# A decoder layer in split float32: every SBUF tile is laid 32 bytes further

## The chip, the core and the metric

The kernel runs on one core of one Trainium2 chip. The metric is the device time of one launch in microseconds (us). Before the change, three runs gave 2425.56, 2427.79 and 2438.43 us, a median of 2427.79.

## The reference, cut to what matters

One decoder layer for 1,024 tokens of width 1,024, all in float32:

```python
f1 = swiglu(rms_norm(h, g1), ffn1_w_in, ffn1_w_out)      # 1024 -> 2 x 2816 -> 1024
h  = h + 0.5 * rms_norm(f1, p1)
u  = rms_norm(h, mix_pre_g)
p_rwkv, p_swa, q_mem, gate_logits = split(u @ w_in)      # 1792 | 768 | 512 | 3 x 1024 columns
y_a = rwkv7_mix(p_rwkv, ...)                             # a recurrence over the tokens
y_b = sliding_window_gqa_sinks(q_s, k_s, v_s, sinks)     # window 128
y_c = memory_cross_attention(q_mem, rms_norm(mem), mem_w_kv)
g_a, g_b, g_c = split(sigmoid(gate_logits + gate_b))
merged = g_a * (y_a @ wb0) + g_b * (y_b @ wb1) + g_c * (y_c @ wb2)
h  = h + rms_norm(merged @ w_out, mix_post_g)
f2 = swiglu(rms_norm(h, g2), ffn2_w_in, ffn2_w_out)
h  = h + 0.5 * rms_norm(f2, p2)
```

## The kernel before, in words

Activations lie feature by feature: a tile of 128 features by 512 tokens (half of the tokens) is 2,048 bytes in each of the 128 partitions. Weights come from HBM in strips of 128 x 1,024 values, 4,096 bytes in each partition, into two buffers named `w_raw` (line 121).

The large products keep float32 accuracy with a cheaper type, float32r. `operand` (lines 125 to 131) casts half a strip to a float32r tile `w_hi` on ScalarE and puts what the cast lost into a tile `w_lo` on VectorE. `split` (lines 248 to 251) does the same for activations, into pairs of tiles of the pool `u`. `mm3` (lines 190 to 196) then multiplies three times: high weights by high activations (L194), high weights by low activations (L195), low weights by high activations (L196). Each of these matmuls streams an activation tile, in most cases 512 columns wide, past 128 x 128 weights; each loads its weights anew.

The smaller products of the mixer (the recurrence in `rwkv_chain`, the two attentions, the sums over a head) use plain float32. The trace counts two matmul instructions for one of these in the program, and one for a float32r matmul or a transpose.

The stages follow one another: the memory's keys and values, the first feed-forward block, the mixer (preparation and inversion for the recurrence, the recurrence itself, attention over memory and over the window, gates, branches), the output projection, the second feed-forward block. In both feed-forward blocks the products of `ffn_in_pair` (names `px`, `py`, `pz`) come first, and those of `ffn_out_one` (`po`) after. `plan` (line 81) lists the strips in the order of use, and `prefetch` makes operands up to eight ahead. A scheduler orders the instructions of each engine by that program and its priorities.

Where a tile lies is settled by the pools. Pools on the left side grow up from byte 16,512 of a partition, pools on the right side grow down from the top; every tile takes a multiple of 32 bytes. On the left stand the constants (pool `consts`: `vecs` with 488 bytes, `ones`, `ident`, `post1`, `post2`), then the weights (pool `w`: `w_raw`, `w_hi`, `w_lo`, `w_sum`), then the pools of each stage. On the right stand the pool `u` with 32 tiles, and the pool `quarters` with the tiles named `acc`, `r2`, `f`, `hid` and `x_re`. In the mixer many stage tiles stand behind constants of odd sizes.

Of the kernel before, what the change touches and what calls it, by code (L numbers as in the profile page):

```python
# [10 lines left out]
F32 = mybir.dt.float32  # L11
# [6 lines left out]
P = 128  # L18
# [58 lines left out]
class Builder:  # L77
# [1111 lines left out]
    def build(self):  # L1189
        nc, tc, io = self.nc, self.tc, self.io  # L1190
        with contextlib.ExitStack() as outer, tc.tile_pool(reuse_waits="tile", name="consts", bufs=1) as cp, \
             tc.tile_pool(reuse_waits="tile", name="w", bufs=1) as self.wpool, \
             tc.tile_pool(reuse_waits="tile", name="pmm", bufs=8, space=bass.MemoryType.PSUM) as self.pmm:
            self.plan()
            self.vecs = cp.tile([P, NVEC], F32, name="vecs")
            nc.scalar.dma_start(self.vecs, io["vecs"])
            self.ones = cp.tile([P, 1], F32, name="ones")
# [14 lines left out]
            vm_d = tc.dram_tile([P, 2, 512], F32, name="vm_d")  # L1212
            hid_d = tc.dram_tile([KF, P, T], F32, name="hid_d")
            first_d = tc.dram_tile([max(FIRST.values()), 2, P, TH], F32, name="first_d")
            self.upool = outer.enter_context(tc.tile_pool(reuse_waits="tile", name="u", bufs=32, side="right"))
            quarters = lambda: tc.tile_pool(reuse_waits="tile", name="quarters", bufs=16, side="right")
            u = self.new_u()
# [122 lines left out]
```

## Time and profile before

| | |
|---|---|
| median of three runs | 2427.79 us (2425.56 to 2438.43) |
| profiled execution, first to last instruction (span) | 2422.9 us |
| TensorE (PE): matmuls busy | 98% of the span, 12,500 matmul instructions |
| weight loads (PEld) busy | 79% |
| VectorE (DVE) busy | 64% |
| ScalarE (ACT) busy | 37% |
| GpSimd (POOL) busy | 4% |
| mean granted TensorE clock | 0.995 |
| DMA | 323.75 MB, mean 134 GB/s |

The profiled execution's own time is its span of 2422.9 us and whatever lies around it; the median of the runs is 4.9 us above the span.

How to read the rows below. PE is a matmul, PEld the weight load that belongs to it; DVE, ACT and POOL are the three vector-like engines. L194 is line 194 of the kernel. `po<-u,w_hi` names the output and the operands; of a matmul the first operand named is the one that streams past the weights. `x640` counts instructions. Matmuls overlap one another in the pipeline, so a matmul's duration is longer than the step from one start to the next; that step is what sets the pace.

### The profile page before, as it was taken

To read this page: it belongs to the slowest core of one execution; us is meant where nothing else is said; L and a number is where in the kernel's file an instruction comes from. 1 tells how busy PE (TensorE), PEld (TensorE's weight loads), DVE (VectorE), ACT (ScalarE), POOL (GpSimd) and SP (SyncE) were. 2 spreads that over 40 slices of the span, in tenths; PEclk is the share of its full clock that TensorE was granted. 3 is DMA by queue.
4 is the path that set the end of the run, shared out by engine and by line. 5 is a ranking of instruction groups with operands and counts; after the bars stand their busy time and mean duration, and the time that the engine had idled before them with its cause. 6 is when DMAs were issued, how large, how long until landed. Compare 5 with 4: busy or idle time off the path is not lost.

```text
span 2422.9 us, 33132 instructions
## 1 busy us (share of the span) xinstructions
PE 2367.7 (98%) x12500; PEld 1926.0 (79%) x12500; DVE 1550.3 (64%) x2563; ACT 895.5 (37%) x1680; POOL 107.7 (4%) x145
## 2 busy tenths in 40 slices
PE   7999999999999999999999999999999999999998
PEld 6878888788888777887777877778887778878888
DVE  8976555654588775993435366575897665564535
ACT  6523333422345533223344464334642233341221
POOL 2000000000000000001210000240000000000000
PEclk9999999999999999999999999999999999999999
DMA  7453222632344244225326434555545432252303
GB/s 253 148 187 114 95 79 79 195 112 84 103 156 146 96 163 168 97 112 177 115 82 209 126 115 136 169 178 170 171 159 177 158 107 91 90 190 97 113 22 105
DMA packets 159615, 323.75 MB, mean 134 GB/s; under 512 B 31296, under 2 KB 61504, under 8 KB 159200
## 3 DMA queue, kind: packets, MB, share of 16 engines
q1 hardware_dynamic: 144000, 294.31, 36.6%
q10 hardware_dynamic: 15456, 27.33, 3.3%
q8 instruction: 98, 1.61, 0.3%
q14 instruction: 61, 0.50, 0.1%
HBM read 231.41 MB, written 89.13 MB: 132 GB/s over the span
## 4 chain that ended last, share of the span: by engine, by line
PE 79%; DVE 10%; DMA 5%; issue 3%; ACT 3%; POOL 0%; ACTq 0%; SPq 0%; DVEq 0%; POOLq 0%
PE po L194 6%; PE po L195 6%; PE po L196 6%; PE px L194 5%; PE px L195 5%; PE px L196 5%; PE pgate L194 3%; PE pgate L196 3%; PE pgate L195 3%; DMA w_raw<-in_ffn_in 2%; PE pz L195 2%; PE pz L194 2%; PE pz L196 2%; DVE w_lo L131 2%; PE pr L196 2%
## 5 line engine op out<-in xcount | busy, mean ns | idle before, releaser
L129 ACT CAST w_hi<-w_raw 128x512 fp32r<-128x512 f32 x560 | 343.2, 620 | 837.5 <-PE po L195 216.6
L131 DVE TENSOR_TENSOR w_lo<-w_raw,w_hi 128x512 fp32r<-128x512 f32 x552 | 387.4, 705 | 165.8 <-ACT w_hi L129 159.3
L194 PE MATMUL po<-u,w_hi 128*128 128x512 f32 (+2 forms) x768 | 288.9, 376 | 2.3 <-DVE acc L492 2.3
L196 PE MATMUL po<-u,w_lo 128*128 128x512 f32 (+2 forms) x768 | 288.2, 375 | 0.0
L195 PE MATMUL po<-u,w_hi 128*128 128x512 f32 (+2 forms) x768 | 288.1, 375 | 0.0
L495 DVE TENSOR_TENSOR acc<-po,acc 128x512 f32<-128x512 f32 (+2 forms) x136 | 89.5, 658 | 177.6 <-PE po L196 177.4
L194 PEld LDWEIGHTS po<-u,w_hi 128*128 128x128 f32 x768 | 144.4, 188 | 29.0 <-DVE acc L492 4.1
L196 PEld LDWEIGHTS po<-u,w_lo 128*128 128x128 f32 x768 | 144.4, 188 | 25.0
L195 PEld LDWEIGHTS po<-u,w_hi 128*128 128x128 f32 x768 | 144.4, 188 | 24.7
L194 PE MATMUL pgate<-u,w_hi 128*128 128x512 f32 x384 | 154.3, 402 | 0.0
L196 PE MATMUL pgate<-u,w_lo 128*128 128x512 f32 x384 | 153.7, 400 | 0.0
L195 PE MATMUL pgate<-u,w_hi 128*128 128x512 f32 x384 | 153.1, 399 | 0.0
L194 PE MATMUL px<-f,w_hi 128*128 128x512 f32 x352 | 138.2, 393 | 6.9 <-DVE u L406 3.8
L195 PE MATMUL pz<-u,w_hi 128*128 128x512 f32 x352 | 136.9, 389 | 0.5 <-DVE u L251 0.5
L195 PE MATMUL px<-u,w_hi 128*128 128x512 f32 x352 | 137.2, 390 | 0.0
L196 PE MATMUL px<-u,w_lo 128*128 128x512 f32 x352 | 137.2, 390 | 0.0
L196 PE MATMUL px<-f,w_lo 128*128 128x512 f32 x352 | 137.1, 390 | 0.0
L195 PE MATMUL px<-f,w_hi 128*128 128x512 f32 x352 | 137.0, 389 | 0.0
L194 PE MATMUL pz<-u,w_hi 128*128 128x512 f32 x352 | 136.9, 389 | 0.0
L196 PE MATMUL pz<-u,w_lo 128*128 128x512 f32 x352 | 136.9, 389 | 0.0
L194 PE MATMUL px<-u,w_hi 128*128 128x512 f32 x352 | 136.9, 389 | 0.0
L260 ACT ACTIVATE sq<-acc 128x512 f32<-128x512 f32 (+2 forms) x104 | 60.9, 598 | 106.2 <-DVE acc L495 88.8
(324 smaller groups left out, 4713.8 us busy)
## 6 DMA issues: line engine op xcount, KB each, us to landing
w_raw<-in_ffn_in SPq DMA_DIRECT2D x110, 512.0 KB
w_raw<-in_win SPq DMA_DIRECT2D x56, 512.0 KB
w_raw<-in_ffn_out SPq DMA_DIRECT2D x52, 512.0 KB
hid_d<-g SPq DMA_DIRECT2D x88, 256.0 KB
hid<-hid_d SPq DMA_DIRECT2D x88, 256.0 KB
gate_d<-gate SPq DMA_DIRECT2D x24, 512.0 KB
pk_d<-pk ACTq DMA_DIRECT2D x4, 2560.0 KB
f<-pk_d SPq DMA_DIRECT2D x16, 640.0 KB
```

Source lines behind the costliest of these rows:

```text
L129: self.nc.scalar.copy(hi, x)
L131: (engine or self.nc.vector).tensor_tensor(lo, x, hi.bitcast(F32), ALU.subtract)
L194: mm(out, wh, xh, start=first, stop=False, **kw)
L195: mm(out, wh, xl, start=False, stop=False, **kw)
L196: mm(out, wl, xh, start=False, stop=last, **kw)
L260: nc.scalar.activation(sq, x, ACT.Square)
L495: self.nc.vector.tensor_tensor(out, ps, out, ALU.add)
```

## The change

Two tiles of 32 bytes in each partition are added, which nothing reads or writes. One, `pad`, is the first tile of the constants and pushes every tile on the left 32 bytes up. The other, `edge`, is the first tile of the right side and pushes every tile there 32 bytes down.

```diff
             self.plan()
+            cp.tile([P, 8], F32, name="pad")
             self.vecs = cp.tile([P, NVEC], F32, name="vecs")
...
             first_d = tc.dram_tile([max(FIRST.values()), 2, P, TH], F32, name="first_d")
+            outer.enter_context(tc.tile_pool(name="edge", bufs=1, side="right")).tile([P, 8], F32, name="edge")
             self.upool = outer.enter_context(tc.tile_pool(reuse_waits="tile", name="u", bufs=32, side="right"))
```

In the two built programs every engine has the same instructions in the same order with the same waits. Of 3,156 tile instances in SBUF, 2,535 lie 32 bytes higher, 616 lie 32 bytes lower, and 5 (constants of the framework) stay. Tiles in PSUM and tensors in HBM stay where they were. What is left of some starting bytes when they are divided by 128:

| tiles | before | after |
|---|---|---|
| `w_raw`, `w_hi`, `w_lo`, `w_sum`; `m1`, `g`, `up` of the feed-forward blocks; memory tiles `mem_x`, `mem_hi`, `mem_lo`; `y` of the last branch | 96 | 0 |
| `u`, `acc`, `r2`, `hid`, `x_re`, and `f` of the feed-forward blocks | 96 | 64 |
| `lora`, `g_up`, `bones`, `center`, `gmask`, `wmask` | 96 | 0 |
| `ident` | 32 | 64 |
| the mixer's stage tiles: `pk`, `f`, `gz`, `bk`, `uv`, `sv`, `z` of the recurrence; `qs`, `sc`, `pt`, `km_in`, `vm_in`, `kd`, `vt`, `cos`, `sin`; `gate`, `att` | 0 | 32 |
| `yin` | 64 | 96 |

So the tiles of the feed-forward blocks and all float32r operands lie at multiples of 64 bytes after the change, and most of the mixer's own tiles, which did so before, no longer do.

## The prediction

> **What bounds the kernel now.** I read the page first, then the table by stretches, then the order of time on TensorE.
>
> ```profile
> span 2422.9 us, 33132 instructions
> PE 2367.7 (98%) x12500; PEld 1926.0 (79%) x12500; DVE 1550.3 (64%) x2563; ACT 895.5 (37%) x1680; POOL 107.7 (4%) x145
> PE 79%; DVE 10%; DMA 5%; issue 3%; ACT 3%; POOL 0%; ACTq 0%; SPq 0%; DVEq 0%; POOLq 0%
> ```
>
> TensorE is busy for 98% of the span, and 79% of the chain that ended last is its work. In whole stretches it never rests, at the full granted clock, with every other engine below it:
>
> ```profile
> 300.00:400.00 100.00, 100.00 (x443) 82.81 (x442) 55.82 (x87) 36.58 (x63) 0.00 (x0) 1.00 0.26 88
> 1000.00:1100.00 100.00, 100.00 (x443) 82.81 (x442) 87.60 (x104) 23.42 (x39) 0.00 (x0) 1.00 0.35 129
> ```
>
> The columns behind the two times are PE, PEld, DVE, ACT and POOL, the granted clock, the DMA share and GB/s. So what counts is the step from one matmul to the next. The order of time on PE from 320 to 330 us has 46 rows, of which these are the first and the last:
>
> ```profile
> 319.72 0.39 PE L194 MATMUL px<-u,w_hi 128*128 128x512 f32 x1
> ...
> 329.92 0.39 PE L194 MATMUL px<-f,w_hi 128*128 128x512 f32 x1
> ```
>
> 45 steps in 10.20 us are 226.7 ns each. Three rows, one for each line of `mm3`, count the float32r matmuls:
>
> ```profile
> 0.00:2423.00 2423.00, 1215.59 (x3136) 590.43 (x3136) 0.99 0.40 134
> 0.00:2423.00 2423.00, 1213.64 (x3136) 590.54 (x3136) 0.99 0.40 134
> 0.00:2423.00 2423.00, 1215.93 (x3136) 590.54 (x3136) 0.99 0.40 134
> ```
>
> 3 x 3,136 = 9,408 of them; at 226.7 ns they would take 2,133 us, nearly the whole span. A change of one nanosecond in this step is worth up to 9.4 us.
>
> **What the change can touch.** It moves no instruction, adds none and adds no wait; the order of work on every engine is the same. Only starting addresses differ: operands of the float32r matmuls go from odd multiples of 32 bytes to multiples of 64, and the mixer's own tiles go the other way. So the question for each engine is whether its instructions care about 32 bytes. The trace of before holds tiles of both kinds, so most of this can be read off.
>
> VectorE and ScalarE: each pair has first an instruction all of whose SBUF tiles lie at odd multiples of 32 (remainder 96 by 128), then one of the same shape whose tiles lie at multiples of 64.
>
> ```profile
> L424 DVE TENSOR_TENSOR g<-g,up 128x512 f32<-128x512 f32 x44 | 30.4, 690 | 3.9 <-ACT g L423 1.4
> L910 DVE TENSOR_TENSOR qs<-qs,cos 128x512 f32<-128x512 f32 x8 | 5.5, 689 | 6.2 <-DMA qs<-att_d 5.9
> L260 ACT ACTIVATE sq<-acc 128x512 f32<-128x512 f32 x88 | 54.3, 631 | 55.8 <-DVE acc L495 38.4 <-DVE sq L264 8.5 <-DVE acc L523 7.8
> L798 ACT ACTIVATE ysq<-y 128x512 f32<-128x512 f32 x8 | 4.8, 629 | 0.1
> ```
>
> 690 against 689 ns and 631 against 629 ns (some of the 88 tiles `sq` lie at multiples of 64 too). I cost both engines at nothing. Even if the 1 or 2 ns were real, they run beside a TensorE that is never idle in the stretches above.
>
> Plain float32 matmuls: `ps_rs<-ident,rsy` streams `ident`, which lies at remainder 32, and `mpv<-mpt,vm_in` streams `mpt`, at remainder 0. Both are 128 columns wide:
>
> ```profile
> L244 PE MATMUL ps_rs<-ident,rsy x100: 271/275/550, 26.2 to 2415.7; 128*128 128x128 f32 x100
> L1033 PE MATMUL mpv<-mpt,vm_in x128: 272/275/377, 1342.5 to 1408.0; 128*128 128x128 f32 x128
> ```
>
> The median is 275 ns for both. So I cost the mixer's tiles, which lose their multiple of 64, at nothing. The bound on the other side stands under the rivals.
>
> DMA: no row tells transfers to the two kinds of tile apart. It is 5% of the chain, about 120 us, so a tenth more or less on each transfer would be 12 us at most; I take nothing, because in the stretches above the DMA engines are busy for a quarter to a third of the time.
>
> The float32r matmuls are what stays open, because in the kernel before every one of them streams a tile at remainder 96. What can be worked out is how much of their step is not columns. Plain float32 matmuls that stream tiles at remainder 0 give the price of a column:
>
> ```profile
> 815.93 1.88 PE L683 MATMUL rk<-m,bones 128*128 128x512 f32 x4
> L683 PE MATMUL rk<-m,bones x16: 590/592/593, 815.9 to 942.8; 128*128 128x512 f32 x16
> 1344.34 1.89 PE L1012 MATMUL msc<-km_in,qm 128*128 128x256 f32 x8
> L1012 PE MATMUL msc<-km_in,qm x64: 379/379/382, 1334.4 to 1400.7; 128*128 128x256 f32 x64
> ```
>
> The first row of each pair is a merged group from first start to last end, the second has the median duration of one. (1.88 - 0.592) / 3 steps = 429 ns for 512 columns; (1.89 - 0.379) / 7 = 216 ns for 256. The difference is 0.832 ns a column, so 429 - 426 = 3 ns is a remainder that belongs to the instruction. If float32r runs its columns at twice that pace, 0.416 ns, 512 columns are 213 ns, and 226.7 leaves a remainder of 13.7 ns. It does not grow with the width. These are the first and the last of 17 rows with 384 columns:
>
> ```profile
> 2353.33 0.33 PE L195 MATMUL po<-u,w_hi 128*128 128x384 f32 x1
> ...
> 2356.11 0.33 PE L196 MATMUL po<-u,w_lo 128*128 128x384 f32 x1
> ```
>
> 2.78 us / 16 = 173.8 ns, less 384 x 0.416 = 159.7, leaves 14.1 ns. So each float32r matmul carries about 13.7 ns that plain float32 at remainder 0 does not show: 10.7 ns more. Either float32r itself or the address is the reason, and no row separates them. The bounds are therefore 0 and 10.7 x 9,408 = 101 us less, and nothing suggests a longer step except the rival below.
>
> I take 0, for three reasons from the rows. First, none of the three comparisons above shows an effect of 32 bytes. Second, plain float32 takes a column in twice the time, so whatever supplies a float32r matmul has half the time for each, and a remainder of its own is what I would expect of it. Third, 13.7 ns are 13.7 / 0.416 = 33 columns, or about 128 bytes. If that were one more piece of an operand that does not start on a piece, the piece would be 128 bytes, and the activations still start at remainder 64 after the change; the extra piece would stay.
>
> A rule of the Trainium skill speaks against the change here too: SBUF — State Buffer, section Specifications, gives lines of 16 bytes and a penalty for crossing to a new one. By that rule a tile at a multiple of 32 starts on a line before and after, and the step stays at 226.7 ns. No row of this trace shows the size of a line.
>
> The sum is then 0 on every engine: the span stays at 2422.9 us and the median at about 2427 us.
>
> **The rivals.**
>
> Rival A, the address makes the remainder. Operands at multiples of 64 bytes let float32r drop to a remainder of 3 ns, a step of 216 ns. For it: the remainder is the same for every width, as a cost at the start of a stream would be. Against it: the three reasons above. It would give 10.7 x 9,408 = 101 us if every float32r matmul were on the path; with the chain's 79% it is 80 us. I take 90: 2338 us, between 2326 and 2348. If only half of the remainder goes (one of two costs, at the weights or at the stream), it is 45 us: 2383 us. The Trainium skill supports A: TensorE: Matmul & The Clock Gate, section "Wait — 56ns, not 53.3ns?", states about 2.5 ns as the fixed cost of back-to-back matmuls. By that rule 11.2 ns of the 13.7 come from somewhere else, which would be 105 us; the 3 ns of the float32 rows agree with it, the float32r rows do not.
>
> Rival B, ending slower: the two reads of TensorE fall out of step. The matmul's stream and the next matmul's weight load read SBUF at the same time. Before, weights and activations have the same remainder, 96; after, 0 and 64. After each stall the trace shows a slower pace that settles only after some ten matmuls:
>
> ```profile
> 61.83 0.40 PE L194 MATMUL py<-r,w_hi 128*128 128x512 f32 x1
> ...
> 64.14 0.39 PE L195 MATMUL px<-u,w_hi 128*128 128x512 f32 x1
> ```
>
> Ten steps in 2.31 us are 231 ns, 4.3 ns over the settled 226.7. If settling needs equal starts and no longer happens, the kernel loses 4.3 x 9,408 = 40 us: about 2468 us. It decides from the point where the settled step is over 228 ns (1.3 x 9,408 = 12 us). Against it: the weight load takes its place beside the stream in plain float32, with operands at remainders 0 and 96 (`m` and `bones`), at a remainder of only 3 ns.
>
> Rival C, the change doesn't do what it says: the streamed activations lie at multiples of 64, but not of 128, and the mixer's tiles lose what the others gain. Where 128 bytes are the unit, only the 192 matmuls that stream `y` in the last branch and the 144 of the memory's keys and values would get faster: 336 x 10.7 ns, under 4 us. That is within no change, and I count it there.
>
> **How the numbers follow.** A measurement of this kernel can tell about 0.5%, 12 us, from no change. No change, C among it: 0.57. A: 0.31, of which 0.19 for the full and 0.12 for the half. B and a loss in the mixer that the rows above don't show: 0.12. The likeliest is no change, 2427 us; its own range is 2420 to 2440, about the spread of the three runs. The range that is to hold 8 in 10 has to take in A, since A has more than 2 in 10: it reaches from 2326 us, the full gain on every matmul, to 2440, and leaves out B.
>
> **What would show it.** In the profile after, the step of `px` and `po` at 512 columns settles it: 226 to 227 ns says that the remainder is float32r's own (or has a unit of 128 bytes), 216 ns says A, 220 to 222 the half, over 228 B. A step that is shorter for `pb<-y` (remainder 0) than for `pb<-u` (64) says 128 bytes. The medians of 690, 631 and 275 ns should stand as they are; if `mpv`, which then streams tiles at remainder 32, went above 275 ns, my costing of the mixer would be wrong. The prediction is wrong if the time leaves 2415 to 2440 us; a shorter time with an unchanged step would mean that DMA or the other engines held the kernel up where I saw none.

## The result, and the profile after

The changed kernel is slower: 2466.11 us median of four runs (2465.31 to 2471.59) against 2427.89 us (2425.56 to 2438.43), a ratio of 1.0151 with a 95% interval of 1.0129 to 1.0174. That is the number of rival B (2468 us), to which the prediction gave a part of 0.12, and it lies outside the range.

The page of the changed kernel, the lines that answer to those of before:

```profile
span 2469.5 us, 33132 instructions
PE 2420.0 (98%) x12500; PEld 1930.6 (78%) x12500; DVE 1553.1 (63%) x2563; ACT 895.5 (36%) x1680; POOL 108.0 (4%) x145
PE 83%; DVE 8%; DMA 4%; ACT 2%; issue 2%; POOL 0%; ACTq 0%; SPq 0%; DVEq 0%; POOLq 0%
```

TensorE is busy 52.3 us longer, and idle for 2469.5 - 2420.0 = 49.5 us instead of 55.2. 52.3 - 5.7 = 46.6 us is the whole difference of the two spans. VectorE and ScalarE worked as long as before (1553 and 896 us against 1550 and 896). The profiled run was the longest of the four, so its difference is larger than the 38.2 us of the medians.

The same two stretches and the order of time on TensorE, of whose 46 rows the first and the last are shown:

```profile
300.00:400.00 100.00, 100.00 (x431) 80.55 (x430) 52.92 (x81) 35.61 (x62) 0.00 (x0) 1.00 0.25 79
1000.00:1100.00 100.00, 100.00 (x430) 80.58 (x429) 97.61 (x106) 21.56 (x37) 0.00 (x0) 1.00 0.27 95
```

```profile
319.69 0.39 PE L195 MATMUL px<-f,w_hi 128*128 128x512 f32 x1
...
330.19 0.40 PE L195 MATMUL py<-r,w_hi 128*128 128x512 f32 x1
```

A stretch of 100 us holds 430 matmuls where it held 443, at the same clock of 1.00. 45 steps now take 10.50 us, 233.3 ns each, where they took 226.7. So the loss is in the step of the float32r matmuls. What did not lose at 512 columns is `pb<-y` in the last branch, whose streamed tile and weights both lie on the left side and moved together. These are the first and the last of 56 rows:

```profile
1632.69 0.39 PE L195 MATMUL pb<-y,w_hi 128*128 128x512 f32 x1
...
1645.16 0.39 PE L196 MATMUL pb<-y,w_lo 128*128 128x512 f32 x1
```

12.47 us / 55 = 226.7 ns. The 48 matmuls of 512 columns for the memory's keys and values, whose operands both moved with the left side too, kept a median step of 227 ns as well. What the prediction costed at nothing stayed as it was:

```profile
L424 DVE TENSOR_TENSOR g<-g,up 128x512 f32<-128x512 f32 x44 | 30.3, 690 | 3.9 <-ACT g L423 1.4
L260 ACT ACTIVATE sq<-acc 128x512 f32<-128x512 f32 x88 | 54.1, 630 | 57.3 <-DVE acc L495 39.8 <-DVE sq L264 8.6 <-DVE acc L523 7.9
L1033 PE MATMUL mpv<-mpt,vm_in x128: 270/275/377, 1370.2 to 1435.6; 128*128 128x128 f32 x128
```

`g` went from remainder 96 to 0 and `mpt` from 0 to 32, and 690, 630 and 275 ns did not move.

### The profile page after: what moved, and what is told of

It is laid out like the page before. It is cut to its first block, busy times and chain, and to the rows that moved or that the text cites. A ratio compares the mean times of both kernels' runs of the same rounds, so it can differ in the third digit from the quotient of the medians.

```text
span 2469.5 us, 33132 instructions
## 1 busy us (share of the span) xinstructions
PE 2420.0 (98%) x12500; PEld 1930.6 (78%) x12500; DVE 1553.1 (63%) x2563; ACT 895.5 (36%) x1680; POOL 108.0 (4%) x145
## 4 chain that ended last, share of the span: by engine, by line
PE 83%; DVE 8%; DMA 4%; ACT 2%; issue 2%; POOL 0%; ACTq 0%; SPq 0%; DVEq 0%; POOLq 0%
PE po L194 6%; PE po L196 6%; PE po L195 6%; PE px L194 5%; PE px L195 5%; PE px L196 5%; PE pgate L194 4%; PE pgate L196 4%; PE pgate L195 3%; PE pz L195 2%; PE pz L196 2%; PE pz L194 2%; PE pr L196 2%; PE pr L194 2%; PE pr L195 2%
## 5 line engine op out<-in xcount | busy, mean ns | idle before, releaser
L194 PE MATMUL po<-u,w_hi 128*128 128x512 f32 (+2 forms) x768 | 293.2, 382 | 2.7 <-DVE acc L492 2.7
L195 PE MATMUL po<-u,w_hi 128*128 128x512 f32 (+2 forms) x768 | 292.3, 381 | 0.0
```

The source lines that it names most:

```text
L194: mm(out, wh, xh, start=first, stop=False, **kw)
L195: mm(out, wh, xl, start=False, stop=False, **kw)
```

## The experiments

The first theory, D: the distance between the start of the streamed tile and the start of the weights decides the step, by some modulus. In the kernel before this distance is 0, in the changed one the stream starts 64 bytes below the weights, and for `pb<-y` it is still 0. The rivals: S, the streamed tile's own start decides (64 is bad, 0 and 96 are good); the weights' own start decides; M, other engines' traffic in SBUF is needed.

**One side alone.** `pad_only` keeps the first half of the change:

```diff
+            cp.tile([P, 8], F32, name="pad")
             self.vecs = cp.tile([P, NVEC], F32, name="vecs")
```

> Only the left side moves 32 bytes up: weights at remainder 0, streamed activations at 96 as before. Theory D: the distance is 96 by 128 instead of 0, so the step is not 226.7 ns; a time of 2445 to 2480 us, and the same as with the right side alone moved. Theory S: the stream has not moved, step 226.7 ns, 2428 us. If the weights' own start decided: 2466 us, and 2428 us with the right side alone.

Measured: 2466.89 us, ratio 1.0154 (1.0138 to 1.0171). This ratio and those that follow are to executions of the kernel before that were taken beside the experiments, with medians of 2430.56 and, for `even_distance` and `distance_64`, 2430.77 us. `edge_only` keeps the second half:

```diff
+            outer.enter_context(tc.tile_pool(name="edge", bufs=1, side="right")).tile([P, 8], F32, name="edge")
             self.upool = outer.enter_context(...)
```

> Only the right side moves 32 bytes down: weights at remainder 96 as before, streamed activations at 64. Theory D: the distance is again 96 by 128, so the same step and time as with the left side alone, 2445 to 2480 us. Theory S: the stream lies at 64 as in the changed kernel, step 233.5 ns, 2466 us. If the weights' own start decided: 2428 us.

Measured: 2469.19 us, ratio 1.0161 (1.0145 to 1.0176). Each half alone costs as much as both. In `pad_only` the streamed tiles have not moved and in `edge_only` the weights have not, so neither start alone decides: S falls with the first, the weights' own start with the second. Both have the same distance, and the same time within their intervals.

**Both on multiples of 128.** `both_on_128` uses `pad` with 32 bytes and `edge` with 96:

```diff
+            outer.enter_context(tc.tile_pool(name="edge", bufs=1, side="right")).tile([P, 24], F32, name="edge")
```

> The left side moves 32 bytes up and the right side 96 bytes down, so that weights and streamed activations both lie at multiples of 128; their distance is 0 by 128 (128 by 256, where the kernel before has 0 by 256). Theory D with a modulus of 128: step 226.7 ns, 2428 us, though every float32r operand moved. With a modulus of 256: not 226.7 ns, a time of 2440 to 2480 us. Theory S: the stream lies at 0, step 226.7 ns, 2428 us. If a multiple of 128 removed the remainder of 13.7 ns: step 216 ns, about 2340 us.

Measured: 2461.47 us, ratio 1.0133 (1.0117 to 1.0149). A modulus of 128 falls, and so does the hope that a multiple of 128 is good in itself. The distance here is 128 bytes, so D needs a modulus of at least 256.

**The steps by themselves.** `steps` issues nothing but streams of 48 matmuls, one for each pair of starts:

```python
w = W0 + a // 4 + (r == 2) * 2048 + (k % 4) * P
x = X0 + b // 4 + (r == 1) * 2048 + (k % 4) * TH % 2048
tc.keep_in_program_order(nc.tensor.matmul(ps, ops[:, w : w + P], ops[:, x : x + TH], start=m == 0, stop=m == n - 1))
```

> A small kernel with nothing but streams of 48 float32r matmuls of 512 columns, one stream for each pair of starting bytes of weights and streamed tile; it leaves the layer's computation out and copies x to the output. Theory D (the distance between the two starts decides, by some modulus of 128 bytes or more): the settled step is 226.7 ns wherever weights and stream start at the same remainder, about 233.5 ns (231 and 236 in turn) for a stream 64 bytes below the weights, and the same for every pair with the same distance, whatever the starts themselves are. Theory S (the streamed tile's own start decides): the step depends on the stream alone, 226.7 ns at remainders 0 and 96 and 233.5 ns at 64 by 128, whatever the weights' start is. Theory M (other engines' traffic in SBUF is needed): with no such traffic every pair has the same step, 226.7 ns or 216 ns.

This small kernel, like the three that follow, ran once, at a granted clock of 1.0. The order of time on TensorE in `steps`. A row is a stream; the name gives the start of the weights after w and of the stream after x, in bytes, with o for 0 and a to i for 1 to 9 (`woxfd` is 0 and 64, `wfdxo` is 64 and 0). The step is the time from a row's start to the next row's start, by 48.

```profile
41.32 11.04 PE L1253 MATMUL woxo<-ops 128*128 128x512 f32 x48
52.20 11.37 PE L1253 MATMUL woxcb<-ops 128*128 128x512 f32 x48
63.40 11.16 PE L1253 MATMUL woxfd<-ops 128*128 128x512 f32 x48
74.40 11.37 PE L1253 MATMUL woxif<-ops 128*128 128x512 f32 x48
85.61 11.36 PE L1253 MATMUL woxabh<-ops 128*128 128x512 f32 x48
96.81 11.40 PE L1253 MATMUL woxafo<-ops 128*128 128x512 f32 x48
108.05 11.35 PE L1253 MATMUL woxaib<-ops 128*128 128x512 f32 x48
119.24 11.35 PE L1253 MATMUL woxbbd<-ops 128*128 128x512 f32 x48
130.43 11.05 PE L1253 MATMUL woxbef<-ops 128*128 128x512 f32 x48
141.31 11.37 PE L1253 MATMUL woxbhh<-ops 128*128 128x512 f32 x48
...
285.97 11.16 PE L1253 MATMUL wfdxabh<-ops 128*128 128x512 f32 x48
296.96 11.35 PE L1253 MATMUL wfdxo<-ops 128*128 128x512 f32 x48
308.15 11.07 PE L1253 MATMUL wifxif<-ops 128*128 128x512 f32 x48
319.06 11.37 PE L1253 MATMUL wifxabh<-ops 128*128 128x512 f32 x48
...
441.73 11.20 PE L1253 MATMUL wafxaf<-ops 128*128 128x512 f32 x48
452.77 11.06 PE L1253 MATMUL wafxho<-ops 128*128 128x512 f32 x48
463.67 11.37 PE L1253 MATMUL wafxo<-ops 128*128 128x512 f32 x48
```

At distance 0 the step is 10.88 us / 48 = 226.7 ns, at 64 it is 11.00 / 48 = 229.2, and at 32, 96, 128, 160, 192 and 224 it is 11.19 to 11.24 us / 48 = 233 to 234 ns. At 256 it is 226.7 again: the modulus is 256. Weights at 64 with the stream at 128 (`wfdxabh`) take 229.0 ns like any distance of 64, and weights at 64 with the stream at 0 (`wfdxo`) 233.1 ns like any distance of 192, the one of the changed kernel. From 100 us on no other engine works in this run, the DMA engines are still, and the steps are the same: M falls. One part of D was not met: with the weights at 16 bytes, which is no multiple of 32, distance 0 (`wafxaf`) takes 11.04 us / 48 = 230 ns and distance 64 (`wafxho`) 10.90 / 48 = 227.1. So what was found for a distance holds for starts at multiples of 32, which all tiles of the layer have.

**The whole layer moved, at an equal distance.** `even_distance` uses `pad` with 32 bytes and `edge` with 224, so that the distance is 0 by 256 again while every tile has moved and the mixer's tiles lie as in the changed kernel:

```diff
+            outer.enter_context(tc.tile_pool(name="edge", bufs=1, side="right")).tile([P, 56], F32, name="edge")
```

> The left side moves 32 bytes up and the right side 224 bytes down: every tile of the layer has moved, weights and streamed activations now lie at multiples of 128, and their distance is 0 by 256 as in the kernel before; the mixer's own tiles lie at odd multiples of 32 as in the changed kernel. Theory D with a modulus of 256: step 226.7 ns, time within 0.3% of 2428 to 2430 us, and so the mixer's tiles cost nothing. If the starts themselves or the mixer's tiles carried part of the loss: 2440 us or more.

Measured: 2429.54 us, ratio 0.9995 (0.9986 to 1.0003). The order of time, 46 rows from first to last:

```profile
319.71 0.39 PE L194 MATMUL pz<-u,w_hi 128*128 128x512 f32 x1
...
329.91 0.39 PE L194 MATMUL px<-u,w_hi 128*128 128x512 f32 x1
```

226.7 ns, the step of before. The whole loss of the change is the distance; the mixer's tiles off their multiples of 64 cost nothing that can be measured.

**A distance of 64.** `distance_64` has the same `pad` and an `edge` of 160 bytes:

```diff
+            outer.enter_context(tc.tile_pool(name="edge", bufs=1, side="right")).tile([P, 40], F32, name="edge")
```

> The left side moves 32 bytes up and the right side 160 bytes down: streamed activations lie 64 bytes above the weights by 256, where the changed kernel has them 64 below (192). Theory D with the small kernel's steps: 228.9 ns, 2.2 ns over the kernel before, which is a third of the changed kernel's 6.7 ns and so about a third of its 38 us: 2438 to 2452 us. If the distance only had to differ from 0: 2466 us.

Measured: 2443.55 us, ratio 1.0055 (1.0036 to 1.0075), a third of the loss as expected, though not by the one step that was expected. Its order of time in the first and in the second feed-forward block, 46 rows each:

```profile
319.66 0.40 PE L196 MATMUL pz<-u,w_lo 128*128 128x512 f32 x1
...
330.16 0.40 PE L196 MATMUL px<-u,w_lo 128*128 128x512 f32 x1
...
2059.70 0.39 PE L194 MATMUL py<-r,w_hi 128*128 128x512 f32 x1
...
2070.00 0.39 PE L194 MATMUL px<-f,w_hi 128*128 128x512 f32 x1
```

10.50 us / 45 = 233.3 ns in the first, 10.30 / 45 = 228.9 ns in the second: products of the same kind at the same distance run in two rhythms. The slower one holds from 218 to 487 us, for some 1,150 matmuls without a stall between them; in the other long stretches the step settles at the 228.9 ns that was expected. So a distance does not name one price; it allows certain rhythms, and which one holds can differ between stretches of one run.

**What makes the remainder.** `steps_loads` and `steps_few` vary the number of weight columns, the width and the type, and let two starts alternate:

```python
        GROUPS.append((f"r_{c}_{n}", "r", (0,), (d,), cols, 512))
...
GROUPS.append(("r_own", "r", (0, 64), (0, 64), 128, 512))
GROUPS.append(("r_next", "r", (0, 64), (64, 0), 128, 512))
```

> Streams of matmuls alone again, the layer's computation left out, x copied to the output. Theory W (the weight load of the next matmul collides in SBUF with the running stream): with 96, 64 and 32 weight columns instead of 128 the remainder over 213.3 ns gets smaller, to about 3 ns at 32 columns, and differs less between distances; where weights and streams alternate between two starts so that each matmul's own distance is 0 but its stream and the next weights are 64 apart, the step is 229 to 234 ns, and where the own distance is 64 but stream and next weights start alike, it is 226.7 ns. Theory O (a matmul's own stream and own weights matter, without a collision): the other way round, and the same remainder for any number of weight columns. Plain float32, at half the pace: 429 ns at every distance by either theory. bfloat16: no forecast, 216 ns if its operands of half the size don't collide.

The order of time in `steps_loads`; `full`, `most`, `half` and `few` have 128, 96, 64 and 32 weight columns, `low` streams 256 columns; the last part of a name is the distance, spelled as above. `f` is plain float32, `b` is bfloat16.

```profile
34.92 11.04 PE L1225 MATMUL r_full_o<-ops 128*128 128x512 f32 x48
45.80 11.17 PE L1225 MATMUL r_full_fd<-ops 128*128 128x512 f32 x48
...
67.99 11.22 PE L1225 MATMUL r_most_o<-ops 128*96 128x512 f32 x48
79.05 11.35 PE L1225 MATMUL r_most_fd<-ops 128*96 128x512 f32 x48
90.24 11.12 PE L1225 MATMUL r_most_aib<-ops 128*96 128x512 f32 x48
101.20 11.20 PE L1225 MATMUL r_half_o<-ops 128*64 128x512 f32 x48
...
134.37 11.27 PE L1225 MATMUL r_few_o<-ops 128*32 128x512 f32 x48
145.47 11.29 PE L1225 MATMUL r_few_fd<-ops 128*32 128x512 f32 x48
...
184.36 5.91 PE L1225 MATMUL r_low_o<-ops 128*128 128x256 f32 x48
190.10 5.62 PE L1225 MATMUL r_low_aib<-ops 128*128 128x256 f32 x48
195.56 11.28 PE L1225 MATMUL r_own<-ops 128*128 128x512 f32 x48
206.69 11.29 PE L1225 MATMUL r_next<-ops 128*128 128x512 f32 x48
217.81 20.76 PE L1225 MATMUL f_full_o<-raw 128*128 128x512 f32 x48
238.41 20.76 PE L1225 MATMUL f_full_fd<-raw 128*128 128x512 f32 x48
...
300.21 10.52 PE L1225 MATMUL b_full_o<-half 128*128 128x512 bf16 x48
310.57 10.52 PE L1225 MATMUL b_full_fd<-half 128*128 128x512 bf16 x48
320.93 10.52 PE L1225 MATMUL b_full_if<-half 128*128 128x512 bf16 x48
```

Both theories fall as they were put. With 32 weight columns the step is 11.10 us / 48 = 231 ns, longer than the 226.7 ns with 128, not shorter as W wants. `r_own` and `r_next` both take 232 ns (11.13 and 11.12 us), where W and O each want 226.7 ns for one of them; that both distances must be 0 at once is not excluded. One part of W came true: with 32 weight columns the step is 231 to 232 ns at all distances tried, so it differs less between them. With 96 the order is another: 228 ns at distance 192 (10.96 us / 48), 230 at 0, 233 at 64. So the number of weight columns has a part in which distance is good, but the time of their load alone does not make the remainder. Plain float32 takes 20.60 / 48 = 429 ns and bfloat16 10.36 / 48 = 216 ns at each of the four distances tried.

> Streams of float32r matmuls alone again, the layer's computation left out, x copied to the output, at four distances (0, 64, 128, 192 bytes): with 128, 32, 16, 8, 4 and 1 weight columns, and with 448, 384, 320 and 256 streamed columns at 128 weight columns; four streams at distance 0 whose common start is 4, 8, 16 or 48 bytes. If reading the weights makes the remainder over 0.4167 ns a column: with one weight column it is near the 2.5 to 3 ns of the other types, a step of 216 ns, and it shrinks on the way there. If float32r carries it by itself: 13 ns or more remain with one weight column, at every distance. If the distance alone decides at full weights: distance 0 is the best at every width. If it is a matter of how a step's length falls in a period: another distance is the best at some widths, as 192 is at 256 columns. Common starts off a multiple of 32 by the distance alone: 226.7 ns for all four.

The order of time in `steps_few`:

```profile
257.26 11.15 PE L1224 MATMUL r_one_o<-ops 128*1 128x512 f32 x48
268.25 11.26 PE L1224 MATMUL r_one_fd<-ops 128*1 128x512 f32 x48
279.34 11.28 PE L1224 MATMUL r_one_abh<-ops 128*1 128x512 f32 x48
```

With a single weight column the step is 10.99 us / 48 = 229 ns at distance 0 and 231 ns at 64. So a remainder stays that float32r carries by itself, even when a single column is loaded. The price of a column follows from two widths: at distance 0 in this run, 48 steps of 512 columns take 10.88 us and 48 of 384 columns 8.32 us, so a column is 2.56 us / 48 / 128 = 0.4167 ns and 512 columns are 213.3 ns. The remainder is what a step takes beyond its columns. The best distance depends on the width: at 256 columns 192 is the best (5.46 us / 48 = 113.8 ns in `steps_loads` against 119.6 at 0), at 448 it was 64 (200 ns against 203), at 320 all four took 147. Common starts of 4, 8, 16 and 48 bytes took 238, 232, 230 and 233 ns at distance 0; so the distance alone does not decide for every start: the equal starts that gave 226.7 ns were 0, 32, 64 and 96. This fits a matter of how a step falls in a period, but no run shows the period itself. Settled, over the last 30 steps of a stream, the remainder at the best distance tried is 6.7 ns at 256 columns and 13.3 ns at 320, 384, 448 and 512: the time of 16 or of 32 columns.

**Is there a better place?** `steps_search` runs the kernel's own order over 256 placements:

```python
w = ((r == 2) * (8192 + wl) + (q % 4) * 512) // 4
x = (18432 + d + (r == 1) * (8192 + xl) + (q % 4) * 2048) // 4
```

> Streams of 48 float32r matmuls alone, the layer's computation left out, x copied to the output: 256 streams in the kernel's own order (high weights twice, then low weights), over eight distances between high weights and high activations (0 to 224 bytes), eight shifts of the low activations against the high ones and four of the low weights against the high ones. Theory F (226.7 ns is the floor for float32r at 512 columns): no stream is faster, and only those with no shift and distance 0 settle there; a version of the kernel that beats the one before by placing tiles is not to be had. Theory G (distance 0 is only one good place of several, as 113.3 against 120.0 ns at 256 columns suggests): some combinations settle below 226.7 ns, at 220 ns or less.

Over the last 30 steps of each stream the best two of the 256 have a mean of 226.7 ns: no shift at distance 0, and low activations shifted by 160 and low weights by 128 at distance 0. 88 streams round to 233 ns, none is below 226.7. The first two rows:

```profile
35.84 11.04 PE L1210 MATMUL saaa<-ops 128*128 128x512 f32 x48
46.73 11.25 PE L1210 MATMUL saab<-ops 128*128 128x512 f32 x48
```

The stream of the kernel before (`saaa`) takes 10.89 us / 48 = 227 ns. The second best holds its rhythm only at the end: over all 48 steps it averages 228.6 ns. G falls among these placements, F holds but for the second best one, and no version that beats the kernel before came out of this.

## Why the prediction was wrong

**The sum for VectorE, ScalarE and the mixer's plain float32** was right: their rows did not move, and `even_distance` (0.9995), in which every tile of the layer lies elsewhere, shows no cost of theirs that can be measured, that of DMA included.

**The sum for float32r** failed at the step "I take 0, for three reasons from the rows": it put the term at nothing and let no price for a longer step into the sum. In its place the runs show 6.6 ns more for each matmul of 512 columns whose operands lie on two sides (233.3 against 226.7), because the distance of the two starts went from 0 to 192 by 256; the three reasons look at each start by itself. The first reason, that three comparisons show no effect of 32 bytes, carried from plain float32 to float32r a property that it does not share: plain float32 takes 429 ns at every distance tried, float32r 226.7 to 234 by the distance. The second, a remainder of float32r's own, is half right: 229 ns with one weight column shows that something stays, but it is not fixed, and the rows after a stall quoted in the prediction (231 ns) had already shown that. The third, a piece of 128 bytes, fell with `even_distance`, whose operands start at multiples of 128 and still take 226.7 ns, and with `both_on_128`, which is slow on such multiples.

**Rival B** had the condition nearly right: weights and streams fall out of an equal start, and the settled step is lost. It took equal starts by 128; it is by 256. The cause that it named, a collision of the stream with the next weight load, is not shown: `r_next` and the 32 weight columns speak against its simple form. Its price per step was too small, 4.3 ns from the pace after a stall against 6.6 ns settled. That its total of 40 us came close to the measured 38 is in part luck. It was counted over all 9,408 matmuls, though 480 are narrower than 512 columns, 240 kept their step (`pb<-y` and the memory's), and some ran at the slow pace in the kernel before too; and TensorE's idle time shrank by 5.7 us. The argument against it, that weights and stream with remainders 96 and 0 live well together in plain float32, is void for the reason above. Its chance of 0.12 and a range ending at 2440 us left it out.

**Rival A** is refuted at 512 columns: no placement tried came below 226.7 ns, the step of the kernel before. The 2.5 ns of the Trainium skill (TensorE: Matmul & The Clock Gate, "Wait — 56ns, not 53.3ns?") agree with the bfloat16 rows, 215.8 less 213.3 ns for 512 columns, and do not hold for float32r.

**The test in the last part** would have misled: `pb<-y` is shorter than `pb<-u`, which was to say that 128 bytes are the unit. It is shorter because its distance to the weights is 0. The rule of 16-byte lines in the Trainium skill (SBUF — State Buffer, section Specifications) gave no effect for starts at multiples of 32; the measurement decides, and shows one.

## What to carry to other kernels

In a kernel that float32r matmuls pace, look at the step from one matmul's start to the next, not at alignment alone: at 512 columns and 128 weight columns, a streamed tile and its weights should start at multiples of 32 bytes with the same remainder by 256, and a small constant added at one end of SBUF can cost 1.5%. A type or an engine that does not care about an address says nothing about one that runs twice as fast. A slower rhythm that shows for ten steps after each stall, as in the kernel before, can be a sign that the settled one rests on a condition; look for it before tiles are moved.

## What the runs showed of the hardware that was not expected

- The step of a float32r matmul of 512 columns and 128 weight columns is 226.7 ns where its two operands start at the same remainder by 256 bytes, 229 ns in most places where the stream lies 64 bytes above, and 232 to 234 ns at the other multiples of 32. With 226.7 the remainder over the 213.3 ns of 512 columns is 13.3 ns, with 233.3 it is 20 ns.
- At one and the same distance (64) two rhythms, 228.9 and 233.3 ns, hold for long stretches of one run.
- At 256 columns the order turns round: distance 192 is the best, with 113.8 ns against 119.6 at distance 0.
- With 32 weight columns or fewer the distance hardly matters: 229 to 232 ns from one column to 32, at the four distances tried. With 96 columns, distance 192 was better than 0 (228 against 230 ns).

What sets the rhythm stays open. The runs exclude that one operand's start decides alone, that other engines are needed, and that the remainder is the time to read the weights; they do not show where the extra nanoseconds are spent.
